# Layer 1's output product: fixed places on VectorE for the row sums and splits of the next pair

## The chip, the core and the metric

The kernel runs on one core of a Trainium2 chip. The core has five engines with a queue of instructions each, worked in order: TensorE (PE; its weight loads are PEld), VectorE (DVE), ScalarE (ACT), GpSimd (POOL) and SyncE (SP, which here only issues DMAs). They meet through semaphores. On-chip memory is SBUF; TensorE writes to the banks of PSUM. The metric is the device time of one execution in microseconds (us), as the median of several.

## What is computed

Two layers over 2048 latent tokens of width 1024 with 256 context tokens. The change lies in the last step of layer 1, the odd one:

```python
def odd_mixer(h, hc, w_in, q_gain, k_gain, rpb, w_out, update_ctx):
    ...
    o = neighborhood_attention(q_x, k_x, v_x, k_c, v_c, rpb)
    y = jnp.dot(o.reshape(h.shape[0], h.shape[1], C_WIDTH) * jax.nn.silu(z_x), w_out)
...
        x = x + gate * y
```

For every tile of 128 tokens this is (attention x gate path) times a weight of 1024x1024, times the gate, added to x.

## The kernel before

All matrix products are made in three parts: both operands are split into a high and a low part (`project_split`: ScalarE writes the high part as F32R, VectorE subtracts it to get the low one), and TensorE adds high x high, high x low and low x high. One product of a 128x512 operand with 512 columns is 4 x 3 = 12 matmuls.

The 16 token tiles of the output run at the end of `odd_attention`. Tiles 0 to 3 are done one by one (`project_steps`). Tiles 4 to 15 are done in six pairs by `seven(t)`, a scheme with seven block products in place of eight. It needs sums and differences of blocks of the weight (T1 to T4, made once by `weight_sums`) and, for each pair, sums and differences of blocks of the two tiles:

- `pair_load(t)` loads both tiles (the gate path z and the attention output from RT1) over SP's queue into tiles called "opt", of which there are 11 in turn; GpSimd multiplies the two (`product`, L1808). So a load can start when the tile 11 back has been read for the last time.
- `operands` gives four steps. "sums" (L1910) makes the operand hS with two VectorE operations and splits it; hA is the split of the first tile; "more" makes two further operands (L1910), and splits one of them, hS4; hB is the split of the second tile. hA, hS, hB and hS4 have one buffer each: the next pair's high part can be written when this pair's products have read it.
- `prod` issues a product of 12 matmuls (L1940), each product after the one before. With the three PSUM banks U, V and W of a pair the products are, in order: 1 U (hA), 2 V (hS), 3 U (hS, added), 4 W (hA), 5 U (hB, added), 6 V (hS4, added), 7 U (hB, added).
- `copy` takes a bank's first state to SBUF on ScalarE: s1 (U after 1) and s5 (V after 2) into "rl" (two buffers), u2 (U after 3) into "rc" (three buffers). These buffers then hold the results.
- `result` adds a bank and a copy on VectorE (L1952), multiplies by the gate (L1953), and GpSimd's queue issues a DMA that adds it to the output (L1959). The last one has no copy (L1950). Results come after products 4 (W), 5 (U), 6 (V) and 7 (U). Product 7 writes to U after the second result has read it.

In the loop over pairs `seven(t)` is a generator with four yields. At each of them one step of the next pair's operands is issued:

```python
            for t in range(PLAIN, NT - NCT, 2):
                if t + 2 < NT - NCT:
                    after = pair_load(t + 2)
                    ops = operands(*after)
                for n, _ in enumerate(seven(t)):
                    if t + 2 < NT - NCT:
                        ops[n]()
```

The order of the source is not the order on an engine: the program is built with a scheduler that simulates time and places each instruction when it thinks its inputs are there. `issue_after(x)` holds back what is issued under it until x has been placed; TensorE's products are held so, VectorE's operations in this loop are not. Under this schedule VectorE's queue, from the last result of tile 3 to pair 4's results, holds: the row sums of pair 6, hB's low part of pair 4, "more" of pair 6, the row sums of pair 8 with hS's low part of pair 6 among them, half of "more" of pair 8, pair 4's first result.

Of the kernel before, what the change touches and what calls it, by code (L numbers as in the profile page):

```python
# [13 lines left out]
ALU = mybir.AluOpType  # L14
# [74 lines left out]
class Kern:  # L89
# [1433 lines left out]
    def odd_attention(self, out, right, left, wout):  # L1523

        nc = self.nc
        self.RT1 = self.scr("RT1", (KD, P, SEQ), F32)
        NR, NC = (len(b) for b in BLOCKS["k"])
        with ExitStack() as es:
# [60 lines left out]
            def scores(ps, k1, k2, q1, q2):  # L1589
                nc.tensor.matmul(ps, k1, q1, start=True, stop=False)  # L1590
                return nc.tensor.matmul(ps, k2, q2, start=False, stop=True)  # L1591
# [101 lines left out]
            def flush(n):  # L1693

                mm = None
                for f, *a in pend[:n]:
                    mm = f(*a)
                del pend[:n]
                for x in late:
                    x[0] -= 1  # L1700
                for x in [x for x in late if x[0] <= 0]:
                    late.remove(x)
                    finish_block(*x[1:])
                return mm

            for j in range(8):
                OA[j] = {}, {}
                for s, (kind, n) in enumerate(steps):
# [19 lines left out]
                    for i in range(2):  # L1728
                        q1, q2 = Q[j, i]
                        if kind == "c":  # L1730
                            for u in range(2):
                                ps = bank()
                                ks, qs = slice(u * P, u * P + P), slice(n * 512, n * 512 + 512)
                                mm = scores(ps[:], kc[j][0][:, i, ks], kc[j][1][:65, i, ks], q1[:, qs], q2[:65, qs])
# [4 lines left out]
                        ps = bank()  # L1739
                        a, m, d = even(c0, w)  # L1740
                        pt = pts[:, i, : nr * w].rearrange("p (r c) -> p r c", r=nr)
                        ps = ps[:, : nr * m].rearrange("p (r c) -> p r c", r=nr)
                        q1, q2 = (q[:].rearrange("d (r c) -> d r c", r=32)[:, r0_ : r0_ + nr, a : a + m] for q in (q1, q2))
                        mm = scores(ps, k1, k2[:65], q1, q2[:65])
                        ps = ps[:, :, d : d + w]
                        for ro, ri, rn in pieces("k", 0, g, r0_, nr):
                            for co, ci, cn in pieces("k", 1, c, c0, w):
                                d = slice(ro, ro + rn), slice(co, co + cn)
                                bias = nc.vector.tensor_tensor(out=pt[:, d[0], d[1]], in0=ps[:, d[0], d[1]],  # L1749
                                                               in1=tabs[j][i][:, ri : ri + rn, ci : ci + cn], op=ALU.add)  # L1750
# [19 lines left out]
                    elif j == 7 and n == 12:  # L1770
                        gate = ones["kt"][0][:].rearrange("p i c -> p (i c)").bitcast(F32)
# [13 lines left out]
                    if j == 7 and n in (14, 15):  # L1785
# [4 lines left out]
                        with self.tc.issue_after(mm.ins):  # L1790
                            for _ in range(n - 11):
                                mm = next(first)
# [23 lines left out]
            y = lambda: self.tl(fp, [P, 512], "rc", bufs=3)  # L1816
            ready = {t: tile(t) for t in (1, 2)}
            with self.tc.issue_after(mm.ins):
                for _ in range(3):
                    mm = next(first)  # L1820
            with self.tc.issue_after(mm.ins):
                mm = flush(4)
# [8 lines left out]
            half = [slice(0, 512), slice(512, D)]  # L1831
# [55 lines left out]
            def whole(x):  # L1887
                return by_k(x[:].rearrange("p i c -> p (i c)"))

            def two(n):  # L1890
                x = self.tl(rp, [P, 2, 16, 64], f"oacc{n}", F32R, bufs=1)
                return [by_k(x[:, i].rearrange("p r c -> p (r c)")) for i in range(2)]

            hA = [whole(self.tl(kp, [P, 2, 512], "kt1", F32R, bufs=2)) for _ in range(2)]
            h4w = whole(ones["kt"][1])
            hS4 = [h4w[:, :h4, :], h4w[:, h4:, :]]
            hS, hB = two(1), two(0)
            first4, last4 = slice(0, h4), slice(h4, KD)

            def pair_load(t):  # L1900

                za, ra = tile(t)
                zb, rb = tile(t + 1)
                product(za, ra)
                product(zb, rb)
                return za, ra, zb, rb

            def operands(za, ra, zb, rb):

                tt = lambda o, x, y, op: nc.vector.tensor_tensor(out=o, in0=x, in1=y, op=op)  # L1910

                def sums():
                    tt(za[:, first4, :], rb[:, first4, :], rb[:, last4, :], ALU.add)
                    tt(za[:, last4, :], za[:, first4, :], ra[:, first4, :], ALU.subtract)
                    self.project_split(za[:], *hS)

                def more():
                    tt(rb[:, first4, :], ra[:, first4, :], rb[:, first4, :], ALU.subtract)
                    tt(zb[:, first4, :], ra[:, last4, :], za[:, last4, :], ALU.subtract)
                    self.project_split(zb[:, first4, :], *hS4)  # L1920

                return [sums, lambda: self.project_split(ra[:], *hA), more, lambda: self.project_split(rb[:], *hB)]

            def seven(t):

                nonlocal mm
                end = t + 2 == NT - NCT
                if end:
                    res = exps([P, 512])
                    self.load(res[:], self.x1[CTX + (t + 1) * P : CTX + (t + 2) * P, :512])  # L1930
                U = self.tl(pp, [P, 8, 64], "o", bufs=4)[:].rearrange("p r c -> p (r c)")
                V, W = bank()[:], bank()[:]
                tile_of = lambda h, n: [x[:, n * h4 : n * h4 + h4, :] for x in h]

                def prod(ps, A, Bk, start):
                    nonlocal mm
                    with self.tc.issue_after(mm.ins) if mm else ExitStack():
                        for k in range(h4):
                            for n, (x, y) in enumerate(((A[0], Bk[k][0]), (A[0], Bk[k][1]), (A[1], Bk[k][0]))):
                                mm = nc.tensor.matmul(ps, x[:, k, :], y, start=start and k == 0 and n == 0, stop=k == h4 - 1 and n == 2,  # L1940
                                                      skip_group_check=True)

                def copy(ps, pool, tag, bufs):
                    x = self.tl(pool, [P, 512], tag, bufs=bufs)
                    self.act(x[:], ps)
                    return x

                def result(ps, x, row, n, y):
                    if x is None:
                        nc.vector.tensor_tensor(out=y[:], in0=ps, in1=gate[:, half[n]], op=ALU.mult)  # L1950
                    else:
                        nc.vector.tensor_tensor(out=y[:], in0=ps, in1=y[:], op=ALU.add)  # L1952
                        nc.vector.tensor_tensor(out=y[:], in0=y[:], in1=gate[:, half[n]], op=ALU.mult)  # L1953
                    dst = out[(t + row) * P : (t + row) * P + P, half[n]]
                    if end and ps is U and x is None:
                        nc.vector.tensor_tensor(out=y[:], in0=y[:], in1=res[:], op=ALU.add)
                        nc.sync.dma_start(dst, y[:])
                    else:
                        nc.gpsimd.dma_start(dst, y[:], accum_op=ALU.add)  # L1959

                prod(U, tile_of(hA, 0), B(0, 0), True)
                s1 = copy(U, lp, "rl", 2)
                prod(V, tile_of(hS, 0), T1, True)
                s5 = copy(V, lp, "rl", 2)
                prod(U, tile_of(hS, 1), T2, False)
                u2 = copy(U, fp, "rc", 3)
                yield
                prod(W, tile_of(hA, 1), B(h4, 0), True)
                result(W, s1, 0, 0, s1)
                yield  # L1970
                prod(U, tile_of(hB, 0), T3, False)
                result(U, s5, 1, 1, s5)
                prod(V, hS4, B(h4, 1), False)
                result(V, u2, 0, 1, u2)
                yield
                prod(U, tile_of(hB, 1), T4, False)
                result(U, None, 1, 0, y())
                yield

            after = pair_load(PLAIN)  # L1980
            ops = operands(*after)
            for n in (1, 0, 2, 3):
                ops[n]()
                if n == 0:
                    for x, place in late_sums:
                        self.project_split(x, *place)
            for t in range(PLAIN, NT - NCT, 2):
                if t + 2 < NT - NCT:
                    after = pair_load(t + 2)
                    ops = operands(*after)  # L1990
                for n, _ in enumerate(seven(t)):
                    if t + 2 < NT - NCT:
                        ops[n]()

    def odd_tail(self, out):
        with ExitStack() as es:
# [104 lines left out]
```

## Time and profile before

| | us |
|---|---|
| median of 3 runs | 3576.32 (3571.68 to 3577.16) |
| profiled execution | 3578.43 |
| its span, first to last instruction | 3576.6 |
| TensorE busy | 3467.2 (97%) |
| VectorE busy | 2391.5 (67%) |
| GpSimd busy | 1247.9 (35%) |
| mean granted TensorE clock | 0.986 |

Times in a view are microseconds from the start of the span. A row of a timeline has start, duration, engine, line, operation, what it writes and reads (numbers of buffers left out), the count, and in brackets the idle time of the engine ahead of it and what ended it. "st" and "o" are PSUM banks (V and W are "st", U is "o"), "kt", "oacc", "q" and others are SBUF tiles that are used again here for operands and weights: hA is "kt" with 1024 columns, hS4 "kt" with 512, hS and hB "oacc"; the gate is "kt" as a second input of a result. Matmuls overlap: a row's duration is longer than the distance to the next.

### The profile page before, as it was taken

How to read it: one execution, taken by the hardware profiler on the slowest of the kernel's cores; microseconds unless marked ns; L12 is line 12 of the kernel's file. 1: busy time of each engine (PE TensorE's matmuls, PEld its weight loads, DVE VectorE, ACT ScalarE, POOL GpSimd, SP SyncE). 2: the span in 40 equal slices, each digit the busy share in tenths (PEclk: the TensorE clock that was granted, in tenths of full speed). 3: DMA queues.
4: the chain of work that ended last, by engine and by line, in shares of the span. 5: the costliest groups of instructions: out<-in, count | busy, mean ns of one | idle time of the engine just before them, and what ended most of it. 6: DMA issues, size and time to landing. Idle time of an engine off the chain costs nothing. (4 is left out here: it accounts for less than half of the span.)

```text
span 3576.6 us, 54014 instructions
## 1 busy us (share of the span) xinstructions
PE 3467.2 (97%) x19532; PEld 2681.2 (75%) x19532; DVE 2391.5 (67%) x4709; ACT 1417.3 (40%) x2562; POOL 1247.9 (35%) x1382
## 2 busy tenths in 40 slices
PE   8999998999999999999999999999899999999989
PEld 6888887888896666665557878888688887555567
DVE  4677655888885777768874345455577784666774
ACT  4444552111113555546663124444322223555532
POOL 1333421100101333322212234333334443888842
PEclk9999999999999999999999999999999999999999
DMA  7555554222215242334526654445744447888674
GB/s 252 143 158 160 150 142 138 73 86 76 87 50 153 72 131 71 117 107 142 161 85 206 212 177 136 138 144 167 228 146 126 145 122 194 221 223 218 192 199 84
DMA packets 377292, 521.52 MB, mean 146 GB/s; under 512 B 34153, under 2 KB 253753, under 8 KB 370866
## 3 DMA queue, kind: packets, MB, share of 16 engines
q1 hardware_dynamic: 329762, 418.42, 40.6%
q0 software_dynamic: 24096, 63.26, 6.8%
q10 hardware_dynamic: 23168, 36.38, 2.9%
q8 instruction: 155, 2.54, 0.3%
q14 instruction: 111, 0.91, 0.1%
HBM read 338.62 MB, written 187.69 MB: 147 GB/s over the span
## 5 line engine op out<-in xcount | busy, mean ns | idle before, releaser
L661 DVE TENSOR_REDUCE mm<-mx 128x1 f32<-128x512 f32 (+1 forms) x656 | 388.3, 627 | 81.2 <-PE mx L660 74.1
L106 ACT ACTIVATE apt<-st 128x1024 f32<-128x1024 f32 (+1 forms) x296 | 300.1, 1015 | 310.2 <-PE st L1130 294.7
L1137 DVE TENSOR_TENSOR acc<-acc,apt 128x1024 f32<-128x1024 f32 x256 | 340.2, 1329 | 80.9 <-ACT apt L106 61.8
L1130 PE MATMUL st<-aq,akh 64*128 64x512 f32 x1728 | 312.8, 410 | 1.1 <-ACT apt L106 0.6
L1040 PE MATMUL av<-apt,av 128*64 128x512 f32 x1152 | 267.4, 602 | 0.0
L1749 DVE TENSOR_TENSOR opt<-st,tab 128x64 f32<-128x64 f32 (+10 forms) x576 | 144.4, 315 | 140.2 <-PE st L1591 63.9
L1630 POOL TENSOR_TENSOR oacc<-oacc,opt 128x576 f32<-128x576 f32 (+5 forms) x192 | 223.4, 1187 | 38.2 <-ACT rl L106 16.6
L660 PE MATMUL mx<-mk,mq 96*128 96x512 f32 (+1 forms) x656 | 236.0, 373 | 0.8 <-DVE mm L661 0.7
L1130 PE MATMUL st<-aq,akl 64*128 64x512 f32 (+1 forms) x1152 | 231.1, 392 | 0.0
L1130 PEld LDWEIGHTS st<-aq,akh 64*128 64x128 f32 x1728 | 153.5, 186 | 83.0 <-ACT apt L106 28.0
L106 ACT ACTIVATE u<-gm 128x352 f32<-128x352 f32 (+1 forms) x140 | 68.4, 496 | 366.4 <-PE gm L131 207.0
L1507 DVE CUSTOM_DVE_ANT_1 mx<-mx,mtab 128x217 f32<-128x217 f32 (+12 forms) x576 | 184.1, 338 | 39.9 <-PE mx L1501 30.7
L1040 PEld LDWEIGHTS av<-apt,av 128*64 128x64 f32 x1152 | 76.6, 137 | 136.5 <-issue 135.5
L106 ACT ACTIVATE opt<-opt 128x930 f32<-128x930 f32 (+8 forms) x130 | 104.4, 805 | 109.0 <-DVE opt L1749 105.5
L660 PEld LDWEIGHTS mx<-mk,mq 96*128 96x128 f32 x656 | 121.2, 188 | 13.5 <-DVE mm L661 1.9
L1130 PEld LDWEIGHTS st<-aq,akl 64*128 64x128 f32 (+1 forms) x1152 | 112.2, 185 | 23.8
L106 ACT ACTIVATE x<-px,modB,modA 128x128 f32<-128x128 f32 x272 | 99.3, 467 | 60.3 <-PE px L339 29.6
L129 PE MATMUL gm<-w1h,hhi 128*128 128x512 f32 x288 | 116.5, 404 | 6.2 <-ACT onat L106 6.2
L129 PE MATMUL gm<-w0h,hhi 128*128 128x512 f32 x288 | 116.2, 404 | 1.9 <-DVE hhi L351 1.9
L130 PE MATMUL gm<-w1l,hhi 128*128 128x512 f32 x288 | 115.1, 400 | 0.0
L210 POOL TENSOR_TENSOR oss<-oss,mhalf 128x8 f32<-128x8 f32 x68 | 113.1, 1664 | 5.1
L131 PE MATMUL gm<-w0h,hlo 128*128 128x512 f32 x288 | 114.2, 397 | 0.0
(579 smaller groups left out, 9692.3 us busy)
## 6 DMA issues: line engine op xcount, KB each, us to landing
q<-Q SPq DMA_DIRECT2D x48, 512.0 KB
H<-x ACTq DMA_DIRECT2D x36, 512.0 KB
adaw<-ada_w SPq DMA_DIRECT2D x64, 256.0 KB
x<-H SPq DMA_DIRECT2D x32, 512.0 KB
wraw<-w_od SPq DMA_DIRECT2D x64, 256.0 KB
K1t<-okt POOLq DMA_DIRECT2D x32, 512.0 KB, 7.5
kt<-K1t SPq DMA_DIRECT2D x32, 512.0 KB
mtab<-rpb_q SPq DMA_DIRECT2D x16, 899.0 KB
```

The source lines that it names most:

```text
L106: return self.nc.scalar.activation(out, in_, func, **kw)
L129: self.nc.tensor.matmul(out, lh(k), rh(k), start=start and j == 0, stop=False)
L130: self.nc.tensor.matmul(out, lh(k), rl(k), start=False, stop=False)
L131: yield self.nc.tensor.matmul(out, ll(k), rh(k), start=False, stop=stop and j == n - 1)
L660: mm = nc.tensor.matmul(ps[:, :w], q[:A_QK, (t % 6) * P : (t % 6) * P + P], k[:A_QK, k0 : k0 + w], start=True, stop=True)
L661: nc.vector.tensor_reduce(out=m[:, t, n : n + 1], in_=ps[:, :w], axis=AX.X, op=ALU.max)
L1040: mm = nc.tensor.matmul(O[j, nb][i * 64 : i * 64 + 64, :w], V[j, kt // TT][:, kt % TT, i * 64 : i * 64 + 64], pts[:, i, :w], start=n == 0, ...
L1130: mm = nc.tensor.matmul(ps[:, o // 64, :w], k[o : o + r, kb, kq], Q[o : o + r, qb, :w], start=m == 0, stop=m == 4)
L1137: added = nc.vector.tensor_tensor(out=acc[:, :, :w], in0=a[:, :, :w], in1=pts[:, :, :w], op=ALU.add)
L1507: nc.vector.tensor_tensor_reduce(out=s, in0=s, in1=tb[:, ri : ri + rn, ci : ci + cn], scale=1.0, scalar=-3e38, op0=ALU.add, op1=ALU.max, a ...
L1630: self.psum = nc.gpsimd.tensor_tensor(out=a, in0=a, in1=pts[:, :, a0 - r0 : a1 - r0, :], op=ALU.add)
L1749: bias = nc.vector.tensor_tensor(out=pt[:, d[0], d[1]], in0=ps[:, d[0], d[1]], in1=tabs[j][i][:, ri : ri + rn, ci : ci + cn], op=ALU.add)
```

## The change

The steps are listed in the order hA, sums, more, hB. The yields of `seven` move, so that one stands after each result, and each step is issued under `issue_after` of the result ahead of it (`done`, the last VectorE operation of that result). For the first pair the order stays as it was, only written with other indices.

```diff
-                return [sums, lambda: self.project_split(ra[:], *hA), more, lambda: self.project_split(rb[:], *hB)]
+                return [lambda: self.project_split(ra[:], *hA), sums, more, lambda: self.project_split(rb[:], *hB)]
...
-                nonlocal mm
+                nonlocal mm, done
...
                 def result(ps, x, row, n, y):
+                    nonlocal done
                     if x is None:
-                        nc.vector.tensor_tensor(out=y[:], in0=ps, in1=gate[:, half[n]], op=ALU.mult)
+                        done = nc.vector.tensor_tensor(out=y[:], in0=ps, in1=gate[:, half[n]], op=ALU.mult)
                     else:
                         nc.vector.tensor_tensor(out=y[:], in0=ps, in1=y[:], op=ALU.add)
-                        nc.vector.tensor_tensor(out=y[:], in0=y[:], in1=gate[:, half[n]], op=ALU.mult)
+                        done = nc.vector.tensor_tensor(out=y[:], in0=y[:], in1=gate[:, half[n]], op=ALU.mult)
...
                 u2 = copy(U, fp, "rc", 3)
-                yield
                 prod(W, tile_of(hA, 1), B(h4, 0), True)
                 result(W, s1, 0, 0, s1)
                 yield
                 prod(U, tile_of(hB, 0), T3, False)
                 result(U, s5, 1, 1, s5)
+                yield
                 prod(V, hS4, B(h4, 1), False)
                 result(V, u2, 0, 1, u2)
                 yield
...
-            ops = operands(*after)
-            for n in (1, 0, 2, 3):
+            ops, done = operands(*after), None
+            for n in range(4):
                 ops[n]()
-                if n == 0:
+                if n == 1:
                     for x, place in late_sums:
                         self.project_split(x, *place)
...
                 for n, _ in enumerate(seven(t)):
                     if t + 2 < NT - NCT:
-                        ops[n]()
+                        with self.tc.issue_after(done.ins):
+                            ops[n]()
```

In the changed program L1952 and L1953 are L1953 and L1954, L1950 is L1951 and L1959 is L1960.

## The prediction

> **What bounds the kernel now.** I read the page of the profile first, then the chain of waits in order of time, then the timelines of single engines around the one place where the chain leaves TensorE. The page says how long the run is and that TensorE is hardly ever idle.
>
> ```profile
> span 3576.6 us, 54014 instructions
> PE 3467.2 (97%) x19532; PEld 2681.2 (75%) x19532; DVE 2391.5 (67%) x4709; ACT 1417.3 (40%) x2562; POOL 1247.9 (35%) x1382
> ```
>
> The execution that was profiled took 3578.43 us, 1.8 beside its span. The chain (start, us, engine, tile, line) shows the end of it: the part of the kernel that the change touches begins near 3440.
>
> ```profile
> 3442.75 9.98 DMA opt<-RT
> 3452.75 0.04 POOLq L1808
> ...
> 3452.89 2.37 POOL opt L1808
> ...
> 3457.02 3.43 DVE opt L1910 x2
> 3460.45 0.60 DVE rl L1952
> ...
> 3461.65 3.28 DVE kt L1268
> ...
> 3465.53 0.61 DVE rl L1952
> ...
> 3466.19 7.88 PE o L1940 x24
> ...
> 3474.07 2.79 PE st L1940 x12
> ...
> 3487.98 5.55 PE o L1940 x24
> ...
> 3507.44 5.55 PE o L1940 x24
> ...
> 3565.82 2.80 PE o L1940 x12
> ```
>
> From 3466.19 to 3568.6 nothing but matmuls of L1940 stands in the chain: a product of 12 takes 2.79, and one pair is 3507.44 - 3487.98 = 19.46, seven products back to back. That stretch can't shrink by reordering VectorE. Ahead of it the chain leaves TensorE for a load, GpSimd's product (L1808), VectorE's row sums (L1910) and results (L1952). TensorE's timeline says what that costs.
>
> ```profile
> 3452.77 0.85 PE L1940 MATMUL st<-kc,kt 128*128 128x512 f32 x3
> 3466.19 0.79 PE L1940 MATMUL o<-wo0h,oacc 128*128 128x512 f32 x1 [12.56 <-DVE rl L1952]
> 3471.15 0.40 PE L1940 MATMUL o<-wo0h,kt 128*128 128x512 f32 x1
> ```
>
> I number a pair's products 1 to 7 in the order of the code (1 hA, 2 and 3 hS, 4 hA, 5 hB, 6 hS4, 7 hB). Pair 4's product 6 ends its issue at 3452.77 + 3 x 0.2325 = 3453.47. Product 7 writes the bank U that VectorE's second result has yet to read (L1952, rl<-o), so it starts 12.72 later. And it runs slowly: 3471.15 - 3466.19 = 4.96 for 12 matmuls, 2.17 above 2.79. The windows (us, busy times, then the granted clock) give the reason: the clock fell to half in the gap and stayed there.
>
> ```profile
> 3457.00:3460.00 3.00, 0.00 (x0) 0.00 (x0) 3.00 (x3) 0.00 (x0) 2.30 (x1) 0.51 0.53 148
> 3468.00:3470.00 2.00, 2.00 (x6) 1.55 (x5) 2.00 (x5) 0.00 (x0) 0.01 (x1) 0.50 1.02 133
> ```
>
> The whole cost of the place is 12.72 + 2.17 = 14.89 us.
>
> **What is taken away.** VectorE works in order, and ahead of pair 4's results it holds the row sums of pair 8, two pairs on:
>
> ```profile
> 3455.28 0.69 DVE L1910 TENSOR_TENSOR opt<-opt 128x512 f32<-128x512 f32 x1 [8.07 <-POOL opt L1808]
> ```
>
> It idles 8.07 for GpSimd's product of tile 9, whose load lands at 3452.75. In the changed program, VectorE's list from pair 4 on reads: hB low | first result (2) | next hA low | second result (2) | next sums (2) | third result (2) | next "more" (2) | next hS low | last result | next hB low, hS4 low. Pair 8's sums now stand one pair later. No instruction is added or removed; TensorE's list and SP's loads keep their order. What moves beside VectorE is ScalarE's high split of hA' (ahead of hS', from a wait on product 4 that it had before), and on GpSimd's queue pair 4's four output DMAs, which go ahead of the product of tile 11. Everything up to 3441 is the same, and the gap's cause is gone, so the most that can be won is 14.89.
>
> **What takes its place.** I follow VectorE through the hand-over from pair 4 to pair 6. Durations come from an undisturbed pair:
>
> ```profile
> 3482.45 0.69 DVE L1952 TENSOR_TENSOR rl<-st,rl 128x512 f32<-128x512 f32 x1 [0.34 <-PE st L1940]
> 3483.18 0.69 DVE L1953 TENSOR_TENSOR rl<-rl,kt 128x512 f32<-128x512 f32 x1
> 3483.79 1.22 DVE L1268 TENSOR_TENSOR kt<-opt,kt 128x1024 fp32r<-128x1024 f32 x1
> ```
>
> So a 128x512 operation costs 0.60 (0.73 when it needs the one before), a low split of 1024 columns 1.14 to 1.22. But VectorE does not run undisturbed here, as three moments of the trace show, GpSimd's row ahead of VectorE's:
>
> ```profile
> 3417.61 2.47 POOL L1808 TENSOR_TENSOR opt<-opt,opt 128x1024 f32<-128x1024 f32 x1 [6.13 <-DMA opt<-RT]
> 3505.40 2.39 POOL L1808 TENSOR_TENSOR opt<-opt,opt 128x1024 f32<-128x1024 f32 x1 [0.90 <-DMA opt<-RT]
> ...
> 3417.74 0.68 DVE L1284 TENSOR_TENSOR rc<-st,kt 128x512 f32<-128x512 f32 x1
> 3418.34 2.28 DVE L1847 TENSOR_TENSOR opt<-opt,opt 128x512 f32<-128x512 f32 x1
> 3505.43 2.91 DVE L1953 TENSOR_TENSOR rl<-rl,kt 128x512 f32<-128x512 f32 x1
> ```
>
> During a GpSimd product, a result that reads a PSUM bank runs on (0.68 at 3417.74), while an operation with two SBUF inputs ends 0.55 after the product does (3418.34 + 2.28 = 3420.62 against 3420.08; 3508.34 against 3507.79). Three products fall into the hand-over, and their loads are not moved by the change:
>
> ```profile
> 3448.56 2.40 POOL L1808 TENSOR_TENSOR opt<-opt,opt 128x1024 f32<-128x1024 f32 x1 [4.21 <-DMA opt<-RT]
> 3452.89 2.36 POOL L1808 TENSOR_TENSOR opt<-opt,opt 128x1024 f32<-128x1024 f32 x1 [1.93 <-DMA opt<-RT]
> 3455.95 3.35 POOL L1808 TENSOR_TENSOR opt<-opt,opt 128x1024 f32<-128x1024 f32 x1 [0.71 <-DMA opt<-RT]
> ```
>
> - First result: product 4 issues its last matmul near 3447.84, so it reads PSUM at 3448.05. Its second half (two SBUF inputs) is held by the first product until 3450.96, done 3451.56. hA' low runs to 3452.7.
> - Second result reads U at 3452.7 to 3453.4. Product 6 ends at 3453.47, so product 7 follows with no wait. Product 1 of pair 6 then starts at 3456.26. Its second half is held until 3455.25, done 3455.85.
> - Sums': first operation to 3456.45, with GpSimd's third product held behind it; that product runs 3456.45 to 3458.85, and the second sum ends 3459.45. hS' high (ScalarE, 1.06) ends 3460.65.
> - Third result to 3460.75, "more" to 3461.95, hS' low to 3463.15.
>
> Product 2 of pair 6 is due at 3456.26 + 2.79 = 3459.05. It needs the high part (3460.75, idle 1.7), does two matmuls and needs the low part (3463.15, idle 1.9). Ten matmuls are left: it ends at 3465.5 instead of 3461.84, a loss of 3.6. Without any holding the same operations would end hS' low near 3457.5, ahead of its use: that is the lower bound, no loss.
>
> The clock adds to this. A window of 3.41 with 0.86 idle was already followed by half clock once:
>
> ```profile
> 3013.34:3016.76 3.42, 2.39 (x12) 1.00 0.46 134
> 3016.76:3020.17 3.41, 2.55 (x10) 1.00 1.02 319
> 3020.17:3023.59 3.42, 3.42 (x11) 0.50 1.06 223
> ```
>
> Here 3.6 of some 4.1 us are idle, so I take one window at half clock, 1.7 us lost; none and two (3.4) are the bounds. The Trainium skill (TensorE: Matmul & The Clock Gate, "Why this matters for your kernels") allows idle gaps of up to about 3 us between bursts; by that rule neither gap of 1.7 or 1.9 would lower the clock and the loss would be 3.6 alone. The row at 3016.76 speaks against it, so I keep the 1.7.
>
> Sum: 14.89 - 3.6 - 1.7 = 9.6 us. Span 3576.6 to 3567.0, the profiled execution 3578.43 to 3568.8; that execution stood 2.1 above the median of 3576.32, so the predicted time is 3576.32 - 9.6 = 3566.7.
>
> Later hand-overs cost nothing. Counted from a pair's product 1, the first result starts at 4 x 2.79 + 0.2 = 11.4, the third result's second half ends at 18.3, "more" at 19.5, hS' low at 20.7; product 2 of the next pair is due at 19.46 + 2.79 = 22.25. GpSimd's products lie outside that stretch: a load takes 4.04 to its product (issue below against 3505.40 above), and its tile is freed by hS' low (next pair's 1.2) or hS4' low (3.7), so the two products run at about 5.2 to 7.6 and 7.7 to 10.1.
>
> ```profile
> 3501.36 0.36 SPq L111 DMA_DIRECT2D opt<-RT  x1
> ```
>
> **The rivals.**
> 1. *No holding at the hand-over; the buffer of the first copy becomes the wait.* Pair 4's first result leaves by a DMA that now stands behind the product of tile 10 (end 3458.35), and its buffer "rl" is wanted by pair 6's copy of product 1 ahead of product 3, due 3461.84.
>
> ```profile
> DMA to landing us min/median/max: 3.6/4.0/6.6
> 3474.11 0.60 ACT L106 ACTIVATE rl<-o 128x512 f32<-128x512 f32 x1 [1.85 <-PE o L1940]
> ```
>
>    3458.35 + 4.0 + 0.6 = 3462.95, a loss of 1.1 (3.7 with 6.6), and the gain is 13.8: 3562.5. For it: the loads could land elsewhere. Against it: three products in 10 us were seen, and VectorE is nearly full there.
> 2. *The clock holds.* The two idle stretches may be cut by a window's border so that each window is over half busy, and the window ahead of the one above had 1.03 idle with no fall after it (the row at 3016.76 has 1.00). Gain 14.89 - 3.6 = 11.3: 3565.0. Against it: 3.6 idle in 4.1 leaves hardly a border at which neither window has 1.7 idle. This is where the Trainium skill's rule leads too.
> 3. *A second hold.* If tile 9's load lands 1.4 earlier, before 3451.56, its product starts ahead of hA' low, which then ends 1.1 after the product instead of ahead of it; the second result and product 7 are late by up to 2.4, perhaps with a further window at half clock (1.7): gain 5.5 to 7.2, about 3570. For it: product 7 has a margin of only 0.1. Against it: the load would have to come at another time than in the trace.
> 4. *Slower: the stall of the first hand-over repeats in all five.* Fixed places put hS' low last, 1.6 ahead of its use. If GpSimd's products fell after 11.4 in each pair, each hand-over would lose 3.6 + 1.7 = 5.3: 26.5 - 14.9 = 11.6 slower, 3588. It decides from 14.9 / 5 = 3.0 per hand-over, and needs loads 3 us later than the rows give.
> 5. *The change doesn't act:* product 7 waits as long for another reason (a load of tile 7 or 9 not in): about 3576. VectorE's list leaves it no place before pair 6.
>
> **How the numbers follow.** Forecast (own range 3564 to 3569) 0.50; rivals 1: 0.15, 2: 0.10, 3: 0.13, 4: 0.06, 5: 0.06. 0.2% is 7.2 us, about what can be told from no change here (the three runs spread over 5.5). Faster is the forecast less 0.05 for its weak end, rivals 1 and 2: 0.70. Same is that 0.05 with rivals 3 and 5, less a hundredth for their tail: 0.23. Slower is rival 4 with that hundredth: 0.07. The range runs from the bound of no stall (3561.4, less 2 for the spread) to rival 3 with two windows at half clock and the spread: 3559.5 to 3575.
>
> **What would show it.** In the changed profile: no TensorE wait over 1 us at pair 4's product 7; a wait of 3 to 4 us in two parts at pair 6's product 2, on ScalarE's and VectorE's oacc; one window at 0.50 after it; VectorE operations of over 2 us at L1954 and L1910 beside L1808; 19.46 for each later pair. It is wrong if TensorE waits at each hand-over, or if product 7 still waits.

## The result, and the profile after

| us | before | changed |
|---|---|---|
| median (12 runs each) | 3574.59 (3566.07 to 3578.61) | 3566.9 (3561.2 to 3569.57) |
| profiled execution | 3578.43 | 3569.04 |
| its span | 3576.6 | 3567.2 |

The ratio to before is 0.9979, with a 95% interval of 0.997 to 0.9988: some 7.7 us faster by the medians, 9.4 by the two spans. The predicted time was 3566.7, for a gain of 9.6.

First TensorE's timeline in the changed kernel, at the place where the 12.56 us wait stood (start, duration, engine, line, operation, output and inputs, count, idle time and what ended it):

```profile
3452.76 0.85 PE L1940 MATMUL st<-kc,kt 128*128 128x512 f32 x3
3453.44 0.49 PE L1940 MATMUL o<-wo0h,oacc 128*128 128x512 f32 x1
...
3456.33 0.40 PE L1940 MATMUL o<-wo0h,kt 128*128 128x512 f32 x1
...
3460.59 0.73 PE L1940 MATMUL st<-q,oacc 128*128 128x512 f32 x2 [1.35 <-ACT oacc L106]
3463.12 3.97 PE L1940 MATMUL st<-q,oacc 128*128 128x512 f32 x10 [1.80 <-DVE oacc L1268]
3466.89 3.17 PE L1940 MATMUL o<-q,oacc 128*128 128x512 f32 x12
```

Pair 4's product 7 follows product 6 with no gap, and pair 6's product 1 starts at 3456.33. Product 2 then waits twice: 1.35 for ScalarE's high part of hS and 1.80 for VectorE's low part. Here is VectorE in the same kernel, and below it GpSimd's products:

```profile
3448.87 2.78 DVE L1954 TENSOR_TENSOR rl<-rl,kt 128x512 f32<-128x512 f32 x1
3451.57 1.21 DVE L1268 TENSOR_TENSOR kt<-opt,kt 128x1024 fp32r<-128x1024 f32 x1
3452.70 0.68 DVE L1953 TENSOR_TENSOR rl<-o,rl 128x512 f32<-128x512 f32 x1
3453.41 2.58 DVE L1954 TENSOR_TENSOR rl<-rl,kt 128x512 f32<-128x512 f32 x1
3455.92 0.68 DVE L1910 TENSOR_TENSOR opt<-opt 128x512 f32<-128x512 f32 x1
3456.63 2.77 DVE L1910 TENSOR_TENSOR opt<-opt,opt 128x512 f32<-128x512 f32 x1
...
3461.85 1.22 DVE L1268 TENSOR_TENSOR oacc<-opt,oacc 128x1024 fp32r<-128x1024 f32 x1
```

```profile
3448.69 2.40 POOL L1808 TENSOR_TENSOR opt<-opt,opt 128x1024 f32<-128x1024 f32 x1 [3.87 <-DMA opt<-RT]
...
3453.04 2.40 POOL L1808 TENSOR_TENSOR opt<-opt,opt 128x1024 f32<-128x1024 f32 x1 [1.95 <-DMA opt<-RT]
3456.06 2.79 POOL L1808 TENSOR_TENSOR opt<-opt,opt 128x1024 f32<-128x1024 f32 x1 [0.62 <-DMA opt<-RT]
```

Each of the three GpSimd products meets one VectorE operation with two SBUF inputs, and that one is held: it takes 2.6 to 2.8 in place of 0.7, and ends 0.5 to 0.6 after the product. The result at 3452.70, which reads a PSUM bank, is not late. So hS low ends at 3463.07, where 3463.15 was worked out. The windows of this kernel (granted clock behind the five busy times) show the half clock, from 3463.94 on, after the waits:

```profile
3459.00:3463.10 4.10, 0.97 (x4) 0.30 (x2) 4.07 (x7) 2.63 (x3) 2.42 (x3) 1.00 0.76 94
3463.94:3467.35 3.41, 3.41 (x10) 2.65 (x9) 1.46 (x2) 0.22 (x1) 0.87 (x1) 0.50 1.03 214
3467.35:3470.76 3.41, 3.41 (x16) 2.79 (x15) 0.00 (x0) 0.98 (x2) 1.53 (x1) 1.00 1.15 292
```

From there the chain of waits is matmuls to the end. One pair takes 3517.53 - 3498.07 = 19.46, as before; only the hand-over from pair 6 is 0.2 longer (3498.07 - 3478.41 = 19.66).

```profile
3478.41 5.75 PE o L1940 x24
...
3498.07 5.55 PE o L1940 x24
...
3517.53 5.55 PE o L1940 x24
```

For the experiments a measure is needed that the rest of the kernel doesn't disturb: executions reach this place some microseconds apart (from 3445.22 to 3456.39 in the nine traces below). I count "the stretch": from the start of the last three matmuls of pair 4's product 6 (st<-kc,kt) to the end of the span. Before it is 3576.6 - 3452.77 = 123.8, in the changed kernel 3567.2 - 3452.76 = 114.4: all of the 9.4 between the two spans came from this stretch. Each stretch below is that of the one profiled execution of its kernel.

### The profile page after: what moved, and what is told of

Its sections match the earlier page's. It is cut to its first block, busy times and chain, and to the rows that moved or that the text cites. A ratio compares the mean times of both kernels' runs of the same rounds, so it can differ in the third digit from the quotient of the medians.

```text
span 3567.2 us, 54003 instructions
## 1 busy us (share of the span) xinstructions
PE 3465.4 (97%) x19532; PEld 2680.1 (75%) x19532; DVE 2400.1 (67%) x4709; ACT 1419.3 (40%) x2562; POOL 1248.8 (35%) x1382
## 4 chain that ended last, share of the span: by engine, by line
PE 80%; DMA 7%; DVE 6%; ACT 2%; POOL 2%; issue 2%; SPq 1%; DVEq 0%; ACTq 0%; POOLq 0%
PE st L1130 10%; PE gm L129 10%; PE gm L130 10%; PE gm L131 10%; PE av L1040 7%; PE mx L660 4%; PE o L1624 2%; PE st L1590 2%; DMA wraw<-w_od 2%; PE pj L129 2%; PE pj L131 2%; PE pj L130 2%; PE o L1940 2%; DMA adaw<-ada_w 1%; PE st L1940 1%
## 5 line engine op out<-in xcount | busy, mean ns | idle before, releaser
L660 PEld LDWEIGHTS mx<-mk,mq 96*128 96x128 f32 x656 | 121.2, 188 | 14.9 <-DVE mm L661 1.9
L130 PE MATMUL gm<-w0l,hhi 128*128 128x512 f32 x288 | 114.6, 398 | 0.0
```

What stands on the lines that cost most here:

```text
L130: self.nc.tensor.matmul(out, lh(k), rl(k), start=False, stop=False)
L660: mm = nc.tensor.matmul(ps[:, :w], q[:A_QK, (t % 6) * P : (t % 6) * P + P], k[:A_QK, k0 : k0 + w], start=True, stop=True)
```

## The experiments

The theory: the change takes away a gap of 14.9 us, and some 5.5 of it come back because GpSimd's products hold VectorE's operations with two SBUF inputs on the way to hS low. In the kernels with added lines the line numbers of results and products are up to four higher. Rivals: the buffers "rl" of the copies are the wait; VectorE has too much to do in one hand-over; the gap went because of the new yields, not of the fixed places.

| kernel | what is other | median (runs) | stretch |
|---|---|---|---|
| before | | 3574.59 (12) | 123.8 |
| changed | | 3566.9 (12) | 114.4 |
| e1 | changed, products later | 3558.84 (7) | 108.9 |
| e2 | changed, no products of tiles 8 to 10 | 3558.4 (1) | 108.9 |
| e3 | changed, places not fixed | 3572.98 (10) | 123.4 |
| e4 | before, products later | 3561.08 (6) | 108.9 |
| e5 | changed, a product doubled | 3565.28 (1) | 117.3 |
| e6 | changed, memsets for products | 3560.84 (1) | 113.9 |
| e7 | changed, no product of tile 9 | 3570.79 (1) | 112.6 |

**e3: the changed kernel without the fixed places.**

```diff
-                        with self.tc.issue_after(done.ins):
-                            ops[n]()
+                        ops[n]()
```

> The changed kernel without the placing under issue_after: the order of the steps and the yields are the new ones, the scheduler may move the steps. VectorE's queue then has pair 8's row sums ahead of pair 4's results again. Theory: the gap of 12 to 13 us at pair 4's product 7 is back, the span is that of before, 3576 to 3577. Rival (the new places of the yields do the work): 3567.

The gap is back, in TensorE's and VectorE's timelines of this kernel:

```profile
3459.54 0.79 PE L1940 MATMUL o<-wo0h,oacc 128*128 128x512 f32 x1 [12.24 <-DVE rl L1953]
```

```profile
3448.63 0.69 DVE L1910 TENSOR_TENSOR opt<-opt 128x512 f32<-128x512 f32 x1 [7.71 <-POOL opt L1808]
```

VectorE again idles 7.7 for the product of tile 9 ahead of pair 4's results. The ratio to before is 0.9997 (0.9984 to 1.001). The absolute 3576 that was expected was missed (span 3569.8), because this execution came to the place 6.3 earlier; the stretch of 123.4 is that of before. The new yields and the order of the steps do nothing by themselves: the fixed places are needed. Whether they would do it with the old order and yields was not run.

**e1: the changed kernel with the products placed later.** `sent` is the last output DMA of a pair, on GpSimd's own queue.

```diff
-                product(za, ra)
-                product(zb, rb)
+                with self.tc.issue_after(sent.ins) if sent else ExitStack():
+                    product(za, ra)
+                    product(zb, rb)
...
-                        nc.gpsimd.dma_start(dst, y[:], accum_op=ALU.add)
+                        sent = nc.gpsimd.dma_start(dst, y[:], accum_op=ALU.add)
```

> The changed kernel, with GpSimd's two products of each later pair placed on its queue behind the last output DMA of the pair two ahead. Holding theory (VectorE operations with two SBUF inputs wait for a running GpSimd product): no product runs while VectorE works through the hand-over from pair 4 to pair 6, hS low ends near 3457.5 and TensorE has no wait at product 2, no half clock after it: span about 5.0 us shorter than the changed kernel's 3567.2, so 3562; no VectorE operation of L1955 or L1911 over 1 us in pair 4's results. Rival (the copy buffer rl is the wait): the same DMA leaves earlier here, so also faster, but the held operations would still be there. Rival (VectorE simply has too much to do in one hand-over): TensorE still waits about 3.6 at product 2, span 3567.

VectorE's timeline of this kernel, at the same operations as above:

```profile
3443.70 0.69 DVE L1955 TENSOR_TENSOR rl<-rl,kt 128x512 f32<-128x512 f32 x1
...
3446.43 0.69 DVE L1955 TENSOR_TENSOR rl<-rl,kt 128x512 f32<-128x512 f32 x1
3447.04 0.68 DVE L1911 TENSOR_TENSOR opt<-opt 128x512 f32<-128x512 f32 x1
3447.76 0.69 DVE L1911 TENSOR_TENSOR opt<-opt,opt 128x512 f32<-128x512 f32 x1
...
3451.01 1.22 DVE L1268 TENSOR_TENSOR oacc<-opt,oacc 128x1024 fp32r<-128x1024 f32 x1
...
3453.88 5.44 DVE L1268 TENSOR_TENSOR kt<-opt,kt 128x512 fp32r<-128x512 f32 x1
```

Nothing is held up to hS low, which starts at 3451.01, and TensorE has no wait from pair 4's product 7 on. The products now hold hS4 low, for 5.44, and nobody waits for it. The stretch is 108.9, the 114.4 less 5.5, so the same VectorE list is no longer too long once it isn't held. The span, 3556.5, is below the 3562 expected because this execution also reached the place 5.2 earlier. Ratio to before 0.9963 (0.9948 to 0.9977): with e4 the fastest of the kernels that leave nothing out.

**e4: the kernel of before with only the products placed later.** The edit is the one above; nothing of the change is in it.

> The kernel of before, with only the placing of GpSimd's products as in the run above and nothing of the change. If the gap of 12.7 us came from pair 8's row sums standing ahead of pair 4's results on VectorE, and those sums come later because their product does, the gap goes without the change, and nothing is held at the hand-over: 14 to 15 us less than the span of before, about 3562. If the order that the change fixes by hand is needed in itself, TensorE waits at pair 4's product 7 or at later pairs: 3567 or more.

Stretch 108.9, ratio 0.9963 (0.995 to 0.9976); the span of 3559.0 is below the 3562 expected because the place was reached 2.7 earlier. Pair 8's row sums can't be placed ahead of a product that isn't issued yet, so they leave VectorE's queue in front of pair 4's results by themselves. VectorE's timeline has pair 4's first result first, and pair 8's row sums behind all four:

```profile
3445.72 0.68 DVE L1954 TENSOR_TENSOR rl<-st,rl 128x512 f32<-128x512 f32 x1
...
3453.72 0.69 DVE L1952 TENSOR_TENSOR rc<-o,kt 128x512 f32<-128x512 f32 x1 [0.90 <-PE o L1941]
...
3460.53 0.69 DVE L1911 TENSOR_TENSOR opt<-opt 128x512 f32<-128x512 f32 x1 [4.64 <-POOL opt L1808]
```

One wait is left that e1 doesn't have, ahead of the stretch: 0.70 at pair 4's product 5, since ScalarE makes hS high of pair 6 before the copy u2.

```profile
3445.08 0.50 PE L1941 MATMUL o<-ov,oacc 128*128 128x512 f32 x1 [0.70 <-ACT rc L106]
```

**e2: the changed kernel without the three products.** It leaves out the multiplication of tiles 8, 9 and 10.

```diff
-                product(za, ra)
-                product(zb, rb)
+                if t not in (8, 10):
+                    product(za, ra)
+                if t != 8:
+                    product(zb, rb)
```

> The changed kernel without GpSimd's products of tiles 8, 9 and 10 (those tiles go on without the multiplication by the gate path); the lists of VectorE, ScalarE and TensorE are the same. Holding theory: hS low of pair 6 ends near 3457.5, no TensorE wait at product 2 of pair 6 above 0.3 us, span about 3562. If the operations of over 2 us have another cause (loads landing, ScalarE, semaphores), they stay and so does the wait of 3.2 us: 3567.

Stretch 108.9 with no wait of TensorE in it: VectorE's list is the same, the products are gone, and so are the 5.5. As in e1, one thing more is other than in the changed kernel: the DMA of pair 4's first result has no product ahead of it and leaves right after the result, at 3444.78.

**e5: one product doubled.**

```diff
                 product(za, ra)
+                if t == 10:
+                    nc.gpsimd.tensor_tensor(out=za[:], in0=za[:], in1=ra[:], op=ALU.mult)
```

> The changed kernel with a second GpSimd multiplication of the same size right behind the product of tile 10, into a tile that is written again before it is read. Counted from the start of the last three matmuls of pair 4's product 6 (st<-kc) to the end of the span, the changed kernel takes 114.5, the one of before 123.9, the one with the products later 108.9. Holding theory: the second row sum of the hand-over is held for another 2.4, TensorE's two waits at product 2 grow from 3.15 to 5.5 together, and the stretch to 117 (119 with a further window at half clock). If the wait has nothing to do with GpSimd's reads, it stays at 114.5.

The stretch is 117.3, as expected. TensorE's two waits are these:

```profile
3454.32 0.73 PE L1942 MATMUL st<-q,oacc 128*128 128x512 f32 x2 [1.47 <-ACT oacc L106]
3458.29 4.64 PE L1942 MATMUL st<-q,oacc 128*128 128x512 f32 x10 [3.23 <-DVE oacc L1268]
```

Together 4.70, not 5.5: the doubled product lets VectorE in between its two halves, and it holds the third result's second half (2.13 long) rather than the row sum for longer. The clock was low for two windows after it (6.8 us by the granted clock, against 3.4 in the changed kernel). The expected 117 came true by two errors that cancel: the waits were forecast 0.8 too long, and the second window at half clock was not in it (it stood in the expectation only as the way to 119).

**e7: without the product of tile 9.** Tile 9 goes on without the multiplication.

```diff
-                product(zb, rb)
+                if t != 8:
+                    product(zb, rb)
```

> The changed kernel without GpSimd's product of tile 9, the middle one of the three (tile 9 goes on without the multiplication by the gate path). Holding theory, step by step: the second result's second half is done at 3454.0, both row sums by 3455.4 ahead of the product of tile 10, which then holds the third result's second half until 3459; hS low ends near 3461.4. So the wait for ScalarE's high part is gone, and one of 1.8 for the low part is left: the stretch is 110.8 to 112.5 (114.5 in the changed kernel). A theory of simply less work on GpSimd would take off a third, 5.6 / 3 = 1.9: 112.6 with both waits still there.

```profile
3464.89 2.60 PE L1941 MATMUL st<-q,oacc 128*128 128x512 f32 x10 [1.65 <-DVE oacc L1268]
...
3485.84 2.61 PE L1941 MATMUL st<-q,oacc 128*128 128x512 f32 x10 [0.92 <-DVE oacc L1268]
```

At pair 6 the wait for the high part is gone and one of 1.65 for the low part is left, as the holding theory had it (1.8). The operation that the product of tile 10 held was not the third result's second half, though, but the one behind it, "more" (at 3460.21, 3.48 for two). The stretch of 112.6 is a shade above its range, and would fit the rival's number; but the rival's two waits are not there. What adds to the stretch is a wait that neither foresaw, 0.92 at pair 8: the product of tile 11 came late in this run, at 3474.22, and hA' low of pair 8 took 3.42 beside it; the product of tile 12, at 3477.62, then held the second result's second half (2.18). That is the slower rival of the prediction in small.

**e6: memsets in place of the products.** Tiles 8 to 10 become zero.

```diff
-                product(za, ra)
-                product(zb, rb)
+                for x, (z, r) in enumerate(((za, ra), (zb, rb))):
+                    if t + x in (8, 9, 10):
+                        nc.gpsimd.memset(r[:], 0.0)
+                        nc.gpsimd.memset(r[:], 0.0)
+                    else:
+                        product(z, r)
```

> The changed kernel with two memsets of the tile in place of each of GpSimd's products of tiles 8, 9 and 10 (these tiles become zero): GpSimd is busy at the same places of its queue but only writes SBUF. If it is GpSimd's reading that holds VectorE's operations with two inputs, none of them is over 1 us in the hand-over, and the stretch is 108.9. If any work of GpSimd on SBUF holds them, they stay long by what the memsets last, and TensorE waits at product 2 as before: 112 to 114.5.

The first half of the expectation came true and the second did not. VectorE isn't held: with a memset running at 3445.35 and 3446.36, its two-input operations take what they take alone.

```profile
3445.35 0.95 POOL L1906 MEMSET opt<- 128x1024 f32 x1 [2.33 <-DMA opt<-RT]
3446.36 0.95 POOL L1907 MEMSET opt<- 128x1024 f32 x1
...
3445.38 0.69 DVE L1914 TENSOR_TENSOR opt<-opt,opt 128x512 f32<-128x512 f32 x1
...
3446.83 0.69 DVE L1958 TENSOR_TENSOR rc<-rc,kt 128x512 f32<-128x512 f32 x1
```

So GpSimd's work on SBUF does not hold VectorE as such; what the memset lacks is the reading. This agrees with the Trainium skill (SBUF — State Buffer, "Who interferes with whom"): a VectorE instruction with two SBUF inputs contends with a GpSimd instruction that reads SBUF, not with one that only writes it. Yet the stretch is 113.9, not 108.9, for another reason:

```profile
3450.34 1.75 POOL L1964 DMA_DIRECT2D out_dram<-rl  x2
...
3456.81 0.60 ACT L106 ACTIVATE rl<-o 128x512 f32<-128x512 f32 x1 [6.43 <-DMA out_dram<-rl]
```

```profile
3457.46 4.29 PE L1944 MATMUL o<-q,oacc 128*128 128x512 f32 x12 [3.05 <-ACT rl L106]
```

The DMA of pair 4's first result still stands behind GpSimd's work on tile 10; the result was done at 3442.02 and the DMA is issued at 3450.34. The copy of product 1 waits for this DMA, which empties its buffer "rl", and product 3 waits for the copy. That is the prediction's rival 1, with a wait of 3.05 at product 3 and about one window's length at half clock after it: 5.0 in all (113.9 - 108.9), where the rival had 1.1, or 3.7 for the longest landing, and no fall of the clock. So ending the hold alone wins back only 0.5 of the 5.5 in this run. In e1 and e2 the DMA leaves right after its result, and both waits are gone. It also follows that the time could not have told the two mechanisms apart: 114.4 with the hold and 113.9 with the buffer.

## Why the prediction was right, point by point

- *The gap, 14.89.* Right. Product 7 of pair 4 follows without a wait, and the three kernels whose stretch holds no wait at all have 108.9: 123.8 - 108.9 = 14.9. e3 shows that it is back without the fixed places, e4 that removing its cause in another way removes as much.
- *VectorE's hand-over.* Right in mechanism and near in size: three operations held, a wait in two parts at product 2. The prediction counted from the moment a matmul is due, the brackets from the end of the matmul ahead. By the prediction's count product 2 started 1.47 late (3460.59 against 3456.33 + 2.79) and its third matmul another 2.07 (3463.12 against 3460.59 + 2 x 0.2325): 3.54 in all, where 1.7 + 1.9 = 3.6 was worked out. Product 3 started at 3466.89; with the clock the delay is 4.98 against the 3461.91 that 3456.33 + 2 x 2.79 gives.
- *The clock.* Right in size: one window at half. The 3.6 idle of some 4.1 were not in one window, though. In the 3.42 from 3457.11 TensorE was busy for 2.13, and the clock stayed; in the 3.41 from 3460.53 it was busy for 1.55, and the half clock began where that stretch ends. The ten matmuls behind the waits took 3466.89 - 3463.12 = 3.77, 1.45 above 10 x 0.2325; product 3 adds 0.2.
- *The sum.* 3.6 + 1.7 = 5.3 was forecast, 5.5 measured (114.4 - 108.9): 3.54 of waits, 1.65 of clock, 0.2 at the next hand-over and 0.1 at pair 4's product 7 (3456.33 - 3453.44 = 2.89, where 2.79 is usual). The gain by the spans was 9.4 for 9.6; by the medians 7.7, where the ratio's interval reaches from 4 to 11 us. That the time itself came out only 0.2 from the forecast is luck: the forecast started from a median of 3576.32 over three runs, twelve runs have 3574.59, and these 1.7 are offset by a gain that is 1.9 smaller by the medians.
- *Later hand-overs cost nothing.* This step was wrong in its ground and nearly right in its result. It took 4.04 from a load's issue to its product and had the products end by 10.1 of the next pair. In the changed kernel the tiles of four loads are freed close together, at the end of VectorE's list, and the loads queue up (SP's and GpSimd's timelines):

```profile
3464.83 2.78 SPq L111 DMA_DIRECT2D opt<-RT  x1
...
3473.60 2.39 POOL L1808 TENSOR_TENSOR opt<-opt,opt 128x1024 f32<-128x1024 f32 x1 [1.97 <-DMA opt<-RT]
```

  8.8 us pass from this issue to the product of the load, that of tile 12. It falls on VectorE's next stretch, and an operation takes 2.89 beside it (3473.66). Two things follow. The second result reads U late, until 3478.28, and product 7 of pair 6 starts behind it at 3478.33: that is where the 0.2 were lost. And hS low of pair 8 ends at 3484.00, just as product 2 starts; the margin of 1.55 is used up, and nothing was lost there only because the first two matmuls of product 2 need the high part alone. e7 shows the margin broken once, for 0.92.
- *The rivals.* Number 1 is real, and hidden behind the holding: e6 uncovers it, at a higher price than it was given. Number 2 fell, the clock did go down. Number 3 didn't come, as the loads came at the same times. Number 4 came near at one hand-over, from pair 6 to 8: there its condition, a product behind the first result's start, was met, but one operation was held and not three. The later hand-overs lost nothing (19.46).

## What to carry to other kernels

A fixed place for work that is needed later takes it out of the way of the queue's urgent operations, but the gain is what the next wait leaves of it; so follow the whole list of that engine up to its last urgent operation, with what other engines hold. Where GpSimd multiplies from SBUF while VectorE works on two SBUF inputs, place GpSimd's work in VectorE's idle time: here this alone, on the kernel of before, took 14.9 off the stretch where the change took 9.4, since it kept the row sums, the hold and the late output DMA out of the way at once. And measure a change of a few microseconds from a fixed point inside the trace, since whole spans differ by more than that from one execution to the next.

## What the runs showed of the hardware

Two idle times of 1.35 and 1.80, parted by two matmuls, were followed by half clock for one window of 3.41; 3.05 in one piece was too (e6), 1.47 and 3.23 for two (e5), while 1.65 alone was not (e7). So no single length of gap decides it in these runs: in the kernel of before, a window of 3.41 with only 0.86 idle was followed by half clock too. The rule that the prediction weighed against its row, the Trainium skill's (TensorE: Matmul & The Clock Gate, "Why this matters for your kernels"), allows gaps up to about 3 us; the measurement decides against it here, since neither gap in the changed kernel was over 1.8. And an output DMA that adds to memory took 6.4 and 8.5 us to land in e6 (pair 4's two copies, with loads beside them), against 3.6 to 6.6 for the "rl" copies before and up to 7.5 in e4:

```profile
DMA to landing us min/median/max: 6.4/7.5/8.5
```
